# A SwiGLU feed-forward on one core: units in four parts, the down projection of one part traced beside the gate and up of the next, and 19 of 22 units by seven block products in four PSUM banks

## The chip, the cores and the metric

The kernel runs on one core of one Trainium2 chip. The time is device microseconds for one execution; the profiled execution is a further one, taken by the hardware profiler. Engines are named as in the profile: PE is TensorE (PEld its weight loads), DVE is VectorE, ACT is ScalarE, POOL is GpSimd, SP is SyncE, which here only issues DMA.

## The reference

Two layers of a decoder trunk over 512 tokens of width 1024, float32. Each layer is a mixer of 16 attention heads of three kinds, a SwiGLU feed-forward, and a gated embedding; a norm stands ahead of each and one at the end. The change is in the feed-forward:

```python
D_FF = 2816
...
    hn = rms_norm(h, norm_ffn[i])
    h = h + (jax.nn.silu(hn @ w_ffn_gate[i]) * (hn @ w_ffn_up[i])) @ w_ffn_down[i]
    gate = jax.nn.sigmoid(rms_norm(h, norm_ple[i]) @ w_ple_gate[i])
    h = h + (p[i] @ w_ple_proj[i]) * gate
```

## The kernel before

**Precision by splitting.** Every float32 operand is split in a high and a low part, and each product is three matmuls (high x high, high x low, low x high: `mm3`, lines 223 to 227). Weights arrive by DMA as float32 (`load_raw`, tile `wraw`, four buffers of 512 KB), ACT casts the high part (line 200, or 451), and DVE or GpSimd subtracts it for the low part (line 203, or 452). The result is a tile `whl`, of which there are five. In the feed-forward the general helper `halves` gives every second subtraction to GpSimd.

**Gate and up.** The 2816 hidden columns are taken in 11 pairs of 128 (`fp` 0 to 10), and a pair has two units, gate and up: 22 units a layer. Unit weights are the stationary operand, the normed activations (512 tokens) the moving one, so a unit gives two 128 x 512 results, transposed. A *plain* unit (tile `gu`) has 8 row blocks x 2 halves x 3 = 48 matmuls of 512 columns. Pair 0 is plain with 256 columns at a time, twice as many, since the second half of the tokens is normed later.

**Units by seven.** `seven` (lines 427 to 478, tile `st`) sees a unit as a 2 x 2 block product and makes it with seven block products instead of eight (Winograd's form). The sums of activations that it needs are built once a layer (`operand_sums`); the sums of weights are made for each unit by DVE (`combine`, line 437, in tile `T`). The products run in the order 1, 7, 5, 2, 6, 4, 3. Each is 4 x 3 = 12 matmuls of 256 columns, 84 in all. Four combinations, seven casts on ACT, three splits on GpSimd (products 1, 2, 3) and four on DVE, three copies of partial results on ACT and five additions on DVE (lines 466 to 477), which read PSUM, go with a unit. Results are tiles `gs`, two a unit, of the tag `p`, which has six buffers.

Pairs 1 to 10 take the plain way where `2 * fp + wi` divides by 3 (`wi` is 0 for gate, 1 for up), which are 7 of 20 units, and the other 13 go by seven. PSUM has eight banks in four tags: d two, s three, t two, o one. Gate units by seven take d, d, s, s and up units s, o, t, t.

**The product and the down projection.** For each pair gate is passed through Silu, DVE multiplies gate and up (line 1222), ACT casts (1223) and GpSimd subtracts (1224): the tile `hid`, which is split and ready to be the stationary operand of the down projection. This is done in two parts: pairs 0 to 5, then the down projection of their 12 row blocks; pairs 6 to 10, then that of their 10. A down projection has two halves of 512 columns (`project`), each with four accumulators, one for each 128 tokens, and each row block needs 4 x 3 = 12 matmuls of 512 columns. The first half uses banks d, d, s, s and the second s, t, t, o. DVE adds the accumulators into `h` (`add_h`, line 1109). Ahead of the last half `between` starts the embedding stage, whose input transposes, splits and loads are traced with a lead of 200 instructions.

**The order.** The program is traced in one order, and a planner then places each instruction on its engine by priority (the place in the trace, or ahead of it in a `prio` block) as tiles and inputs come free in its own reckoning. `weave` traces several generators in turn, by the share of each that is done; the mixer uses it. Engines run their own queues in order and wait for one another by semaphores, PE's included. SP issues the loads.

Of the kernel before, what the change touches and what calls it, by code (L numbers as in the profile page):

```python
# [10 lines left out]
F32 = mybir.dt.float32  # L11
# [8 lines left out]
P = 128  # L20
# [22 lines left out]
def hybrid_trunk_kernel(  # L43
# [28 lines left out]
    def bank(tag, shape=(P, 512), dt=F32, name=None):  # L72
        bufs = {"d": 2, "s": 3, "t": 2, "o": 1}[tag]
        return ps.tile(list(shape), dt, name=name or f"ps_{tag}", tag=tag, bufs=bufs)
# [44 lines left out]
    def run(*gens):  # L119
        for g in gens:  # L120
            for _ in g:
                pass
# [68 lines left out]

    turn, lo_turn = [0], [3]

    def load_raw(view, k, c):
        raw = wpool.tile([P, 1024], F32, name="wraw", tag="wraw", bufs=4)
        nc.sync.dma_start(raw[:, :k * c].rearrange("p (k c) -> p k c", k=k), view)
        return raw

# [8 lines left out]
        halves(raw, whl, lo, n)  # L207
        return whl

    def weights(w, kts, c0, c, per):  # L210


        step = min(1024 // c // per * per, len(kts))
        for i in range(0, len(kts), step):
            n = min(step, len(kts) - i)
            src = w[kts[i] * P:(kts[i] + n) * P, c0:c0 + c].rearrange("(k p) c -> p k c", p=P)
            raw = load_raw(src, n, c)
            for j in range(0, n, per):
                t = split(raw, j * c, per * c).rearrange("p t (k c) -> p t k c", c=c)
                for kk in range(per):  # L220
                    yield t[:, 0, kk], t[:, 1, kk]
# [4 lines left out]
        te.matmul(acc, lhsT=ll, rhs=rh, start=False, stop=stop, skip_group_check=True)  # L226
        return i

    def project(act, w, kts, c0, c, evac, tags="ddss", tail=2):

        pack = c <= 256
        if pack:
            b2 = [bank(t, (P, 2, 256), name=f"acc{j}") for j, t in enumerate(tags[:2])]
            accs = [b2[tt // 2][:, tt % 2, :c] for tt in range(NT)]
        else:
            accs = [bank(t, name=f"acc{tt}")[:, :c] for tt, t in enumerate(tags)]
        n = len(kts)
        first = None  # L240
        ws = []
        for i, wt in enumerate(weights(w, kts, c0, c, 2 if pack else 1)):
            k = kts[i]
            if i >= n - tail:
                ws.append((k, wt))
                continue
            for tt in range(NT):
                start = i == 0 and not (pack and tt % 2)
                if i == 0 and pack and tt % 2:
                    with tc.issue_after(first):  # L250
                        mm3(accs[tt], act(k, 0, tt), act(k, 1, tt), *wt, False, False)
                else:
                    m = mm3(accs[tt], act(k, 0, tt), act(k, 1, tt), *wt, start, False)
                    if i == 0:
                        first = m.ins
            yield 12 * c
        for tt in range(NT):
            for j, (k, wt) in enumerate(ws):
                start = n == tail and j == 0
                if start and pack and tt % 2:  # L260
                    with tc.issue_after(first):
                        mm3(accs[tt], act(k, 0, tt), act(k, 1, tt), *wt, False, j == tail - 1)
                else:
                    m = mm3(accs[tt], act(k, 0, tt), act(k, 1, tt), *wt, start, j == tail - 1)
                    if start:
                        first = m.ins

            for t in () if pack and tt % 2 == 0 else (tt - 1, tt) if pack else (tt,):
                with prio(OFE):
                    evac(t, accs[t])  # L270
            yield 3 * tail * c
# [152 lines left out]
            return xact(4 * kh + k, half)[:, t * 256:(t + 1) * 256]  # L424
        return left

    def seven(left, w, c0, tags, done):


        raw = [load_raw(w[kh * 512:(kh + 1) * 512, c0:c0 + 256].rearrange("(k p) c -> p k c", p=P), 4, 256)  # L430
               .rearrange("p (k c) -> p k c", k=4) for kh in range(2)]
        b11, b12, b21, b22 = (raw[i][:, :, j * P:(j + 1) * P] for i in range(2) for j in range(2))
        T, acc, part = {}, {}, {}

        def combine(n, a, b):
            T[n] = t = f(swtile("T")).rearrange("p (k c) -> p k c", k=4)
            ve.tensor_tensor(t, a, b, op=ALU.subtract)
            return t

        def right(n):  # L440
            if n in (1, 2, 3):
                return (b11, b21, b22)[n - 1]
            return combine(n, *{7: lambda: (b22, b12), 5: lambda: (b12, b11), 6: lambda: (b22, T[5]),
                                4: lambda: (b21, T[6])}[n]())

        out = [ptile(f"gs{j}") for j in range(2)]
        for n in (1, 7, 5, 2, 6, 4, 3):
            src = right(n)
            whl = wpool.tile([P, 2, 560], F32R, name="whl", tag="whl", bufs=5)[:, :, :512] \
                .rearrange("p t (k c) -> p t k c", k=4)  # L450
            se.activation(whl[:, 0], src, AF.Copy)  # L451
            (ge if n in (1, 2, 3) else ve).tensor_tensor(whl[:, 1], src, f(whl[:, 0]), op=ALU.subtract)  # L452

            a = {1: 0, 6: 0, 2: 1, 7: 2, 4: 2, 5: 3, 3: 3}[n]
            if a not in acc:
                acc[a] = bank(tags[a], name=f"st{a}")[:, :256]
            for k in range(4):
                mm3(acc[a], whl[:, 0, k], whl[:, 1, k], left(n, 0, k), left(n, 1, k),
                    k == 0 and n in (1, 2, 7, 5), k == 3 and n in (6, 2, 4, 3))
            with prio(OFE):  # L460
                if n in (1, 7):
                    part[n] = eftile("part")
                    se.activation(part[n], acc[a], AF.Copy)
                elif n == 5:
                    part[n] = eftile("part")
                    ve.tensor_tensor(part[n], part[7], acc[a], op=ALU.add)
                elif n == 2:
                    ve.tensor_tensor(out[0][:, :256], part[1], acc[a], op=ALU.add)
                elif n == 6:
                    ve.tensor_tensor(out[1][:, 256:], part[5], acc[a], op=ALU.add)  # L470
                    part[n] = eftile("part")
                    se.activation(part[n], acc[a], AF.Copy)
                elif n == 4:
                    ve.tensor_tensor(out[0][:, 256:], part[6], acc[a], op=ALU.add)
                    done(0, out[0])
                else:
                    ve.tensor_tensor(out[1][:, :256], part[6], acc[a], op=ALU.add)
                    done(1, out[1])

    allk = list(range(KD))  # L480

# [722 lines left out]
    def feed_forward(i, add_h, between):  # L1204
# [7 lines left out]
        def units(fp):  # L1212
# [21 lines left out]

            for wi, w in enumerate((w_ffn_gate[i], w_ffn_up[i])):

                if fp and (2 * fp + wi) % 3:
                    seven(left[0], w, fp * 256, ("ddss", "sott")[wi], (gate_done, up_done)[wi])
                    continue
                accs = [bank(t, name=f"gu{wi}{j}") for j, t in enumerate(("dd", "ss" if fp == 0 else "to")[wi])]  # L1240
                ws = enumerate(weights(w, allk, fp * 256, 256, 2))
                first = []
                if fp == 0:

                    ws = list(ws)
                    part(w, accs, ws, slice(0, 256))
                    with tc.issue_after(first[1]):
                        part(w, accs, ws, slice(256, 512))
                else:
                    part(w, accs, ws, slice(0, 512))  # L1250
                for j in range(2):
                    if wi:
                        up_done(j, accs[j])
                    else:
                        gate[j] = sg = etile("sg")
                        se.activation(sg, accs[j], AF.Silu)
                if fp == 0 and wi == 0:
                    left.append(operand_sums(xact))


        parts = range(0, 6), range(6, NF // 2)
        for fps in parts:
            for fp in fps:
                units(fp)
            end = fps is parts[-1]
            kts = list(range(2 * fps[0], 2 * fps[-1] + 2))
            for c, tags in ((0, "ddss"), (512, "stto")):
                if end:
                    if c:
                        between()  # L1270
                    else:
                        load_gain(norm_ple[i])
                run(project(hact, w_ffn_down[i], kts, c, 512, add_h(c, end), tags=tags,
                            tail=4 if end and c else 2))


    def layer_embedding(i):
# [164 lines left out]
```

## Time and profile before

| | |
|---|---|
| Median of 3 runs | 1540.3 us (1536.8 to 1544.35) |
| Profiled execution, its own time | 1536.46 us |
| Its span, first to last instruction | 1534.5 us |
| Mean granted TensorE clock | 0.997 |
| Instructions | 25780, of them 9562 matmuls |
| DMA | 134.74 MB, mean 88 GB/s |

The page gives an engine's busy time as a share of the span. Matmuls are pipelined, so that a busy PE says that matmuls are under way, not that they could not be closer together; the spacing of their starts says that. The timeline gives starts and durations in us from the start of the span.

### The profile page before, as it was taken

The numbers are of one execution on the slowest core, as the hardware profiler recorded it, in microseconds if no ns is written. First come the engines' busy times: TensorE is split into PE (matmuls) and PEld (weight loads), VectorE is DVE, ScalarE is ACT, GpSimd is POOL, SyncE is SP. The second block draws the span as 40 slices with busy tenths as digits, with TensorE's granted clock in tenths as the row PEclk, the third lists the DMA queues.
The fourth block names the chain that finished last, engine by engine and source line by source line (L and its number), as shares of the span: only waits on it lengthen the run. The fifth ranks groups of instructions, "written<-read, shape, count | busy, mean of one in ns | idle before, by whom it ended". The sixth has DMA issues, their size and how long they took to land.

```text
span 1534.5 us, 25780 instructions
## 1 busy us (share of the span) xinstructions
PE 1482.6 (97%) x9562; PEld 1305.5 (85%) x9562; DVE 988.7 (64%) x1910; ACT 813.3 (53%) x1743; POOL 649.1 (42%) x675
## 2 busy tenths in 40 slices
PE   6999999998999999999999999999899999999998
PEld 6898887878999899988988888778699988998888
DVE  7577868769775267624376878786787733674253
ACT  5477678555454244533365767776455532454243
POOL 3413455454545244432224235555444532455223
PEclk9999999999999999999999999999999999999999
DMA  5521321131433324331225131112122332324321
GB/s 181 134 63 43 84 69 35 49 97 42 124 97 111 96 79 123 118 127 64 83 70 145 52 83 50 54 37 83 56 89 91 106 109 89 111 90 144 110 70 56
DMA packets 114461, 134.74 MB, mean 88 GB/s; under 512 B 6864, under 2 KB 91936, under 8 KB 114336
## 3 DMA queue, kind: packets, MB, share of 16 engines
q1 hardware_dynamic: 114336, 133.10, 28.6%
q8 instruction: 76, 1.25, 0.3%
q14 instruction: 49, 0.40, 0.1%
HBM read 122.59 MB, written 2.10 MB: 81 GB/s over the span
## 4 chain that ended last, share of the span: by engine, by line
PE 81%; DVE 8%; ACT 4%; POOL 3%; issue 2%; DMA 1%; SPq 0%; POOLq 0%; ACTq 0%; DVEq 0%
PE acc L224 6%; PE acc L225 6%; PE acc L226 6%; PE st L225 6%; PE st L226 6%; PE st L224 6%; PE gu L225 4%; PE gu L226 4%; PE gu L224 4%; PE pTp L892 2%; PE sc L871 2%; PE no L1088 2%; PE accr L224 2%; PE accr L225 2%; PE ge L224 2%; PE accr L226 2%
## 5 line engine op out<-in xcount | busy, mean ns | idle before, releaser
L203 POOL TENSOR_TENSOR whl<-wraw,whl 128x512 fp32r<-128x512 f32 (+2 forms) x196 | 267.0, 1367 | 439.1 <-ACT whl L200 412.1
L200 ACT ACTIVATE whl<-wraw 128x512 fp32r<-128x512 f32 (+2 forms) x312 | 195.3, 631 | 249.9 <-PE acc L226 135.0
L203 DVE TENSOR_TENSOR whl<-wraw,whl 128x512 fp32r<-128x512 f32 x116 | 104.8, 904 | 167.2 <-ACT whl L200 166.8
L452 POOL TENSOR_TENSOR whl<-wraw,whl 128x512 fp32r<-128x512 f32 x78 | 115.8, 1491 | 144.4 <-ACT whl L451 144.3
L224 PE MATMUL acc<-whl,hid 128*128 128x512 f32 x352 | 139.1, 395 | 0.0
L225 PE MATMUL acc<-whl,hid 128*128 128x512 f32 x352 | 139.0, 395 | 0.0
L226 PE MATMUL acc<-whl,hid 128*128 128x512 f32 x352 | 138.8, 394 | 0.0
L225 PE MATMUL gu<-xT,whl 128*128 128x512 f32 (+1 forms) x352 | 125.0, 355 | 0.0
L226 PE MATMUL gu<-xT,whl 128*128 128x512 f32 (+1 forms) x352 | 124.8, 355 | 0.0
L224 PE MATMUL gu<-xT,whl 128*128 128x512 f32 (+1 forms) x352 | 124.6, 356 | 0.0
L452 DVE TENSOR_TENSOR whl<-T,whl 128x512 fp32r<-128x512 f32 x104 | 100.3, 971 | 30.1 <-ACT whl L451 29.8
L225 PE MATMUL st<-X,whl 128*128 128x256 f32 x416 | 116.9, 281 | 0.0
L224 PE MATMUL st<-X,whl 128*128 128x256 f32 x416 | 116.6, 280 | 0.0
L226 PE MATMUL st<-X,whl 128*128 128x256 f32 x416 | 116.6, 280 | 0.0
L884 POOL TENSOR_SCALAR p<-p,rc,gt 128x128 f32<-128x128 f32 (+3 forms) x128 | 79.3, 629 | 72.7 <-DVE rc L882 28.8
L879 ACT ACTIVATE p<-sc,mx 128x128 f32<-128x128 f32 (+3 forms) x160 | 83.4, 532 | 10.2 <-DVE mx L876 7.6
L897 ACT ACTIVATE pT<-pTp 128x512 fp32r<-128x512 f32 (+2 forms) x120 | 61.8, 526 | 49.8 <-PE pTp L892 48.5
L451 ACT ACTIVATE whl<-T 128x512 fp32r<-128x512 f32 x104 | 64.3, 625 | 44.7 <-PE gu L226 24.1
L225 PE MATMUL st<-xT,whl 128*128 128x256 f32 x312 | 87.6, 281 | 0.0
L226 PE MATMUL st<-xT,whl 128*128 128x256 f32 x312 | 87.5, 280 | 0.0
L224 PE MATMUL st<-xT,whl 128*128 128x256 f32 x312 | 87.5, 280 | 0.0
L898 DVE TENSOR_TENSOR pT<-pTp,pT 128x512 fp32r<-128x512 f32 (+2 forms) x120 | 70.6, 596 | 24.9 <-ACT pT L897 23.9
(337 smaller groups left out, 4630.9 us busy)
## 6 DMA issues: line engine op xcount, KB each, us to landing
wraw<-in_w_ffn_gate_dram SPq DMA_DIRECT2D x44, 512.0 KB, 3.5
wraw<-in_w_ffn_up_dram SPq DMA_DIRECT2D x44, 512.0 KB, 4.1
wraw<-in_w_ffn_down_dram SPq DMA_DIRECT2D x44, 512.0 KB, 3.7
wraw<-in_w_in_dram SPq DMA_DIRECT2D x36, 512.0 KB, 3.7
wraw<-in_w_out_dram SPq DMA_DIRECT2D x16, 512.0 KB, 3.7
wraw<-in_w_ple_gate_dram SPq DMA_DIRECT2D x16, 512.0 KB, 3.4
sw<-nq SPq DMA_DIRECT2D x32, 128.0 KB, 2.4
wraw<-in_w_in_dram SPq DMA_DIRECT2D x8, 280.0 KB, 2.9
```

Of the source, the lines that this page charges most:

```text
L200: se.activation(whl[:, 0], raw[:, lo:lo + n], AF.Copy)
L203: eng.tensor_tensor(whl[:, 1], raw[:, lo:lo + n], f(whl[:, 0]), op=ALU.subtract)
L224: i = te.matmul(acc, lhsT=lh, rhs=rh, start=start, stop=False, skip_group_check=True)
L225: te.matmul(acc, lhsT=lh, rhs=rl, start=False, stop=False, skip_group_check=True)
L226: te.matmul(acc, lhsT=ll, rhs=rh, start=False, stop=stop, skip_group_check=True)
L451: se.activation(whl[:, 0], src, AF.Copy)
L452: (ge if n in (1, 2, 3) else ve).tensor_tensor(whl[:, 1], src, f(whl[:, 0]), op=ALU.subtract)
L871: te.matmul(s[:, c:c + w], lhsT=lhsT, rhs=rhs, start=(j == 0), stop=False, skip_group_check=True)
L879: se.activation(e[:, u * n:(u + 1) * n], s[:, u * n:(u + 1) * n], AF.Exp, bias=mx[:, u:u + 1], accum_out=sm[:, u:u + 1])
L884: ge.tensor_scalar(e[:, u * n:(u + 1) * n], e[:, u * n:(u + 1) * n], rc[:, u:u + 1], gates[u] if gates else 1.0, op0=ALU.mult, op1=ALU.mult)
L897: se.activation(hi, src, AF.Copy)
L898: ve.tensor_tensor(lo, src, f(hi), op=ALU.subtract)
```

## The change

The feed-forward is cut in four parts, pairs 0 to 2, 3 to 5, 6 to 8 and 9 to 10, instead of two. The first part's units are traced alone. The units of each further part are woven with the down projection of the part ahead of it, a product of a unit and a row block of the down projection at a time, by share. The last part's down projection stands alone at the end. For the weave `seven` and `units` become generators, and `down` is a generator with the old body.

All units by seven use banks s, s, s, o. The down projection uses d, d, t, t in both halves, and plain units use d, d and t, t. Of pairs 1 to 10 only the up unit of pair 1 stays plain, so that 19 of 22 units go by seven.

The down weights are loaded one row block at a time (256 KB, tile `wrow`) into the six buffers of the tag `p`, which the results of `seven` use as well, instead of two at a time (512 KB) into `wraw`.

```diff
-    def load_raw(view, k, c):
-        raw = wpool.tile([P, 1024], F32, name="wraw", tag="wraw", bufs=4)
+    def load_raw(view, k, c, one=False):
+        raw = ptile("wrow") if one else wpool.tile([P, 1024], F32, name="wraw", tag="wraw", bufs=4)
...
-    def weights(w, kts, c0, c, per):
+    def weights(w, kts, c0, c, per, one=False):
-        step = min(1024 // c // per * per, len(kts))
+        step = 1 if one else min(1024 // c // per * per, len(kts))
...
-            raw = load_raw(src, n, c)
+            raw = load_raw(src, n, c, one)
...
-    def project(act, w, kts, c0, c, evac, tags="ddss", tail=2):
+    def project(act, w, kts, c0, c, evac, tags="ddss", tail=2, one=False):
...
-    def seven(left, w, c0, tags, done):
+    def seven(left, w, c0, done):
...
-                acc[a] = bank(tags[a], name=f"st{a}")[:, :256]
+                acc[a] = bank("ssso"[a], name=f"st{a}")[:, :256]
...
                     ve.tensor_tensor(out[1][:, :256], part[6], acc[a], op=ALU.add)
                     done(1, out[1])
+            yield 12 * 256
...
-                if fp and (2 * fp + wi) % 3:
-                    seven(left[0], w, fp * 256, ("ddss", "sott")[wi], (gate_done, up_done)[wi])
+                if fp and (fp, wi) != (1, 1):
+                    yield from seven(left[0], w, fp * 256, (gate_done, up_done)[wi])
                     continue
-                accs = [bank(t, name=f"gu{wi}{j}") for j, t in enumerate(("dd", "ss" if fp == 0 else "to")[wi])]
+                accs = [bank(t, name=f"gu{wi}{j}") for j, t in enumerate(("dd", "tt")[wi])]
...
-        parts = range(0, 6), range(6, NF // 2)
-        for fps in parts:
-            for fp in fps:
-                units(fp)
-            end = fps is parts[-1]
+                yield 48 * 512
+
+        def down(fps, end=False):
             kts = list(range(2 * fps[0], 2 * fps[-1] + 2))
-            for c, tags in ((0, "ddss"), (512, "stto")):
+            for c in (0, 512):
                 if end:
                     if c:
                         between()
                     else:
                         load_gain(norm_ple[i])
-                run(project(hact, w_ffn_down[i], kts, c, 512, add_h(c, end), tags=tags,
-                            tail=4 if end and c else 2))
+                yield from project(hact, w_ffn_down[i], kts, c, 512, add_h(c, end), tags="ddtt",
+                                   tail=4 if end and c else 2, one=True)
+
+        parts = range(0, 3), range(3, 6), range(6, 9), range(9, NF // 2)
+        for n, fps in enumerate(parts):
+            streams = [(chain(*[units(fp) for fp in fps]), len(fps) * 42 * 1024)]
+            if n:
+                streams.append((down(parts[n - 1]), len(parts[n - 1]) * 24 * 1024))
+            weave(*streams)
+        run(down(parts[-1], True))
```

## Rows read from the trace of the kernel before

**Rows 1.** The page: engines over the whole span; below, the last chain by engine.

```profile
PE 1482.6 (97%) x9562; PEld 1305.5 (85%) x9562; DVE 988.7 (64%) x1910; ACT 813.3 (53%) x1743; POOL 649.1 (42%) x675
...
PE 81%; DVE 8%; ACT 4%; POOL 3%; issue 2%; DMA 1%; SPq 0%; POOLq 0%; ACTq 0%; DVEq 0%
```

**Rows 2.** Windows, first layer's feed-forward: length; PE, PEld, DVE, ACT, POOL busy; clock; DMA.

```profile
345.36:376.53 31.17, 26.33 (x209) 25.80 (x208) 29.37 (x27) 15.25 (x26) 13.04 (x12) 0.95 0.16 51
376.53:479.05 102.52, 102.52 (x734) 96.36 (x733) 77.52 (x104) 54.08 (x102) 54.52 (x38) 1.00 0.33 100
479.05:545.64 66.59, 66.59 (x290) 54.18 (x289) 19.56 (x26) 16.18 (x26) 19.41 (x14) 1.00 0.32 101
545.64:649.58 103.94, 103.94 (x700) 95.68 (x698) 68.70 (x92) 50.82 (x95) 50.90 (x35) 1.00 0.35 107
649.58:708.58 59.00, 58.06 (x259) 46.40 (x258) 18.59 (x30) 22.36 (x45) 20.61 (x23) 1.00 0.32 109
```

**Rows 3.** Timeline of PE: the first matmul of four blocks that follow one another.

```profile
376.53 0.28 PE L224 MATMUL st<-xT,whl 128*128 128x256 f32 x1
...
386.43 0.39 PE L224 MATMUL gu<-xT,whl 128*128 128x512 f32 x1
...
397.50 0.28 PE L224 MATMUL st<-xT,whl 128*128 128x256 f32 x1
...
417.28 0.39 PE L224 MATMUL gu<-xT,whl 128*128 128x512 f32 x1
```

**Rows 4.** Groups by line, whole span: busy us, mean ns, then idle before and releasers.

```profile
L452 POOL TENSOR_TENSOR whl<-wraw,whl 128x512 fp32r<-128x512 f32 x78 | 115.8, 1491 | 144.4 <-ACT whl L451 144.3
...
L452 DVE TENSOR_TENSOR whl<-T,whl 128x512 fp32r<-128x512 f32 x104 | 100.3, 971 | 30.1 <-ACT whl L451 29.8
...
L203 POOL TENSOR_TENSOR whl<-wraw,whl 128x512 fp32r<-128x512 f32 (+2 forms) x196 | 267.0, 1367 | 439.1 <-ACT whl L200 412.1 <-DVE dup L500 10.2 <-PE cmp L607 6.4
...
L203 DVE TENSOR_TENSOR whl<-wraw,whl 128x512 fp32r<-128x512 f32 x116 | 104.8, 904 | 167.2 <-ACT whl L200 166.8
...
L437 DVE TENSOR_TENSOR T<-wraw,T 128x512 f32<-128x512 f32 x52 | 53.8, 1034 | 1.2
...
L437 DVE TENSOR_TENSOR T<-wraw 128x512 f32<-128x512 f32 x52 | 45.5, 877 | 26.7 <-DMA wraw<-in_w_ffn_gate_dram 17.0 <-DMA wraw<-in_w_ffn_up_dram 8.9
...
L1224 POOL TENSOR_TENSOR hid<-gs,hid 128x512 fp32r<-128x512 f32 x28 | 40.4, 1460 | 29.6 <-ACT hid L1223 29.6
...
L1109 DVE TENSOR_TENSOR h<-h,acc 128x512 f32<-128x512 f32 x32 | 21.9, 686 | 14.8 <-PE acc L226 14.8
...
L1223 ACT ACTIVATE hid<-gs 128x512 fp32r<-128x512 f32 x28 | 16.9, 624 | 23.3 <-DVE gs L1222 23.3
...
L1222 DVE TENSOR_TENSOR gs<-gs,gs 128x512 f32<-128x512 f32 x12 | 13.4, 1114 | 0.1
...
L474 DVE TENSOR_TENSOR gs<-part,st 128x256 f32<-128x256 f32 x26 | 10.8, 414 | 1.3
```

**Rows 5.** The splits of units by seven (line 452): ns min/median/max, first and last start.

```profile
L452 DVE TENSOR_TENSOR whl<-T,whl x104: 677/693/1797, 375.5 to 1389.2; 128x512 fp32r<-128x512 f32 x104
...
L452 POOL TENSOR_TENSOR whl<-wraw,whl x78: 1291/1322/1766, 369.4 to 1390.4; 128x512 fp32r<-128x512 f32 x78
```

**Rows 6.** The page's DMA issues: count, KB each, median us from issue to landing.

```profile
wraw<-in_w_ffn_down_dram SPq DMA_DIRECT2D x44, 512.0 KB, 3.7
...
wraw<-in_w_in_dram SPq DMA_DIRECT2D x8, 280.0 KB, 2.9
```

**Rows 7.** Timeline at the first layer's feed-forward end: a transpose on PE, additions and split on DVE.

```profile
702.26 0.44 PE L382 MATMUL xnT<-ident,xn 128*128 128x128 f32 x2 [0.40 <-DVE h L1109]
...
705.28 0.68 DVE L1109 TENSOR_TENSOR h<-h,acc 128x512 f32<-128x512 f32 x1
...
710.24 0.67 DVE L1109 TENSOR_TENSOR h<-h,acc 128x512 f32<-128x512 f32 x1
...
717.16 0.69 DVE L390 TENSOR_TENSOR xT<-xnT,xT 128x512 fp32r<-128x512 f32 x1
```

More of the change, by code (lines that the diff above doesn't have):

```diff
@@ L241, in project @@
         ws = []
-        for i, wt in enumerate(weights(w, kts, c0, c, 2 if pack else 1)):
+        for i, wt in enumerate(weights(w, kts, c0, c, 2 if pack else 1, one)):
             k = kts[i]
```

## Prediction

> **What bounds the kernel now.** I read the page's engine shares first. TensorE is busy for 97% of the span, VectorE for 64%, and the chain that ended last runs over TensorE for 81% [rows 1]. The 97% says only that matmuls overlap one another; whether TensorE ever waits is read from where the matmuls start. So I cut one layer's feed-forward into stretches at the first matmul of each block [rows 2]: 345.36 is the first gate matmul of unit pair 0, 376.53 the first seven-product matmul, 479.05 the first down projection, 545.64 pair 6, 649.58 the second down projection. From 376.53 to 649.58 TensorE has no hole and the granted clock is 1.00. Only the opening stretch (4.8 us idle, waiting for the norm) and the last (0.9 us) have any, and the change works at neither hole. The second layer repeats the pattern.
>
> Then the price of a unit [rows 3]. A unit by seven products starts at 376.53 and the next block at 386.43: 9.90 us for 84 matmuls of 256 columns. A plain unit runs from 386.43 to 397.50: 11.07 us for 48 of 512 columns. Two units by seven in a row take 19.78 us, 9.89 each. Now rebuild the stretches: the first has seven units by seven and three plain, 7 x 9.89 + 3 x 11.07 = 102.4 us against 102.52; the other has six and four, 103.6 against 103.94. Nothing but matmul starts is left in them. So feed-forward time here is a sum of matmul pitches, and only fewer or shorter matmuls can shorten it.
>
> **The change, part by part.** *Six units per layer go from plain to seven products* (13 of 22 becomes 19 of 22). Each saves 11.07 - 9.89 = 1.18 us of TensorE; twelve of them save 14.1 us. That is the ceiling: no other matmul disappears, and the down projection keeps its 576 per layer at 66.59 / 288 = 0.231 us.
>
> The Trainium skill has a figure that speaks against this ("TensorE: Matmul & The Clock Gate", Back-to-back issue gap): a sustained stream is said to cost about 131 ns per matmul at 512 columns and 81 ns at 128, so that narrow matmuls are dear. By it even 81 ns would make a unit by seven 84 x 0.081 = 6.8 us against 48 x 0.131 = 6.3 us, and the change would lose. The trace disagrees: 0.231 and 0.118 us.
>
> The break-even is a 256-column pitch of 48/84 = 0.57 of the 512-column one, and rows 3 give 0.51 (9.90/84 against 11.07/48). I give a loss by pitch no chance worth counting.
>
> *What VectorE must do for it.* This is the real question, because a unit by seven costs VectorE [rows 4] four combinations (two at 0.877, two at 1.034), four splits at 0.971 and five evictions at 0.414 us: 9.78 us beside 9.89 us of TensorE. Alone, with the gate-up product on top, units by seven are bound by VectorE. Before, every third unit was plain and gave VectorE time to catch up. Now the down projection is to do that. Per layer, pairs 3 to 10 (16 units) run beside the down projection of pairs 0 to 8: TensorE 16 x 9.89 + 9 x 11.10 = 258.1 us. VectorE: 16 x 9.78 = 156.5; 16 products of gate and up at 1.114 = 17.8; 36 splits of down weights, every other one on VectorE, 18 x 0.904 = 16.3; 24 additions into h at 0.686 = 16.5. Sum 207.1 us, 80%. In the stretch from 376.53 it is 77.52 / 102.52 = 76% [rows 2], and nothing waits. GpSimd: 48 x 1.491 + 18 x 1.367 + 16 x 1.460 = 119.5 us, 46%, against 54.52 / 102.52 = 53%. ScalarE stays near half. So on the averages the cover is as good as before, and I cost it at nothing. If the cover goes, for instance in pair 2 where two units by seven stand alone, VectorE needs 19.6 + 2.2 us against 19.8; but pairs 0 to 2 are the same work in the same order as now, and there 397.50 to 417.28 ran without a wait.
>
> The additions into h double, from 16 to 32 a layer; they are in the sum above.
>
> *Four banks instead of eight.* Each unit by seven now takes the same s, s, s, o, so an accumulator must be evicted before the next unit opens it. The tightest is the o bank: product 3, the last of a unit, closes it, and the next unit opens it with its product 5, two products (2.8 us) later. The eviction takes 0.414 us plus what runs ahead on VectorE. Below: one operation of 0.69 us, 1.1 us in all, no wait. Above: two at the slowest split, 1.80 us [rows 5], 4.0 us, so 1.2 us for each of 38 units, 46 us. In the woven stretch a down step of 12 matmuls (2.77 us) falls between every three or four products and widens the slack. The median split is 0.693 us [rows 5], so I take nothing and keep the upper end for a rival.
>
> *Down on the banks d, d, t, t in both halves.* Before, the two halves had different banks. Now the second half's tile 3 opens 9 matmuls (2.1 us) after the first half's tile 3 ended; the addition into h takes 0.69 us plus at most one slow operation of 1.80 us, 2.5 us. So 0 to 0.4 us at each of 14 seams, 0 to 5.6 us; other streams' matmuls stand ready, so I take 0.
>
> *The t banks at the layer's end.* The next norm's transposes need t. Now the first of them goes into the middle of the down projection, at 702.26, between the matmuls of tiles 1 and 2 [rows 7]. With tiles 2 and 3 themselves in t, it can't go before tile 2 is added, which now ends at 705.96: 3.7 us later at worst. At best nothing, because what ends the phase is tile 3 (added at 710.24, its last operand written at 717.85 [rows 7]), and without transposes in between tile 3 ends earlier. Between 0 and 3.7 us a layer I take 1.5, nearer the end that the last operand supports: 3 us in all. The preparation of the embedding inputs is traced in the same place with the same lead; its ScalarE and VectorE work lies in the last stretch, where they are busy 22.36 and 18.59 of 59.00 us [rows 2], and that stretch now has 22 us of down projection left instead of 55. I count it inside the same 3.7 us.
>
> *Loads.* 44 down loads of 512 KB become 88 of 256 KB on the same queue, into the six p tiles that they share with the results of the units by seven (up to four live). A load lands in at most 2.9 us (the 280 KB row, [rows 6]), the cast and split take 0.63 (as the 0.624 of the hidden cast, rows 4) + 1.367: 4.9 us a slot, and one is wanted every 258.1 / 36 = 7.2 us. One slot would do; nothing.
>
> *Last down part.* It has four steps of rows instead of ten. Its rows 20 and 21 need the last hidden pair: eviction 0.414 + product 1.114 + cast 0.624 + GpSimd 1.460 = 3.6 us [rows 4], under 24 matmuls of rows 18 and 19 (5.5 us). Nothing.
>
> **Sum.** The profiled execution took 1536.5 us (span 1534.5). 1536.5 - 14.1 + 3.0 = 1525.4. The median of the three runs is 1540.3, 3.8 above it, so the forecast for the median is 1529 us, 0.7% faster. A difference under 0.5% (7.7 us) is about what a measurement of this kernel can't tell from no change.
>
> **The rivals.** *A, the forecast*: matmul pitches are saved and little is given back: -14.1 plus 0 to 8 us, or 2 us less if tile 3's chain gains: 1524 to 1534 (both bounds of the seams and the t banks together, 5.6 + 7.4 = 13 us, would be 1539, inside the range below). Chance 0.65. For it: the holes are absent now and VectorE's share hardly rises.
>
> *B, the four banks*: TensorE waits at the opening of a unit for an eviction queued behind one slow VectorE operation. At 0.3 us for each of 38 units it gives back 11.4 us: 1540.3 - 14.1 + 11.4 = 1538. At 0.37 us the gain is gone. For it: the banks halve, and an operation ahead can take 1.80 us. Against: the slack of 2.8 us. Chance 0.22, all within 0.5%.
>
> *C, VectorE becomes the bound, and the kernel slower.* Of its 207.1 us, 162 operations with both operands in SBUF (128 in units by seven, 16 products, 18 splits) take 157.3 us, 0.97 us on average; alone they take 0.69 and beside GpSimd up to 1.80 [rows 5]. TensorE's 258.1 us is reached when the average is (258.1 - 49.8) / 162 = 1.29, the gain is eaten at 1.33, and at 1.40 the layer loses 18.5 us: 1540.3 - 14.1 + 37 = 1563. For it: combinations and splits of all units now lean on VectorE. Against: GpSimd's share falls from 53% to 46%. Chance 0.08.
>
> The Trainium skill says why these stretch ("SBUF — State Buffer", Who interferes with whom): a VectorE instruction with two SBUF inputs and a GpSimd one that reads SBUF exclude each other for the whole instruction. The spread in rows 5 agrees. Taken as one resource by that rule, the stretch from 376.53 has 68 x 0.69 + 37 x 1.29 = 94.6 of 102.5 us and the woven one 162 x 0.69 + 82 x 1.29 = 217.6 of 258.1: the rule speaks against C.
>
> *D, the weave doesn't happen*: the instruction order is settled by a planner, and if it runs the down steps ahead as their inputs allow, the units by seven stand alone at the end. Then VectorE sets them: 16 x 9.78 + 17.8 = 174.3 against 158.2 us, 16 us a layer; 1540.3 - 14.1 + 32 = 1558. Against: in rows 3 the units run in the order in which they are traced. Chance 0.05.
>
> **How the numbers follow.** The time is A's, 1529. The range takes A and B and leaves out C and D (0.13): 1523 to 1541. Faster by over 0.5% means under 1532.6; A gives 0.62 of its 0.65 there, its upper end and B give 0.25 within 0.5%, C and D 0.13 slower.
>
> **What would show it.** Right: 38 x 84 = 3192 matmuls of units by seven where there were 2184, at 0.118 us pitch, no TensorE hole in the woven stretch, VectorE near 80% there, its splits near 0.97 us, and about 7 us less per layer from the first gate matmul to the embedding's first one. Wrong: holes before product 1, 7 or 5 of a unit released by an eviction (B); splits above 1.3 us and TensorE waiting for them (C); long runs of one stream alone (D); a later last operand of the norm (my 3 us).

## The result, and the profile after

The changed kernel takes 1583.3 us (median of four runs, 1578.9 to 1587.1) against 1540.5 us for the kernel before beside it: 1.0278 times as long, 95% interval 1.0260 to 1.0295. The forecast was 1529 us in a range of 1523 to 1541. The profiled execution took 1586.0 us, with a span of 1584.2 us.

The page of the kernel after, with its engines over the span, the last chain by engine, three groups of TensorE and the row of the new load:

```profile
PE 1490.8 (94%) x9994; PEld 1324.2 (84%) x9994; DVE 1091.2 (69%) x2074; ACT 835.3 (53%) x1815; POOL 680.7 (43%) x687
...
PE 60%; DVE 9%; DMA 9%; POOL 8%; ACT 7%; issue 5%; SPq 1%; POOLq 0%; ACTq 0%; DVEq 0%
...
L224 PE MATMUL st<-X,whl 128*128 128x256 f32 x608 | 170.9, 281 | 1.3 <-DVE gs L477 1.3
...
L224 PE MATMUL acc<-whl,hid 128*128 128x512 f32 x352 | 128.8, 407 | 26.9 <-ACT whl L200 26.7
L225 PE MATMUL acc<-whl,hid 128*128 128x512 f32 x352 | 142.3, 404 | 10.2 <-POOL whl L203 8.0
...
wrow<-in_w_ffn_down_dram SPq DMA_DIRECT2D x88, 256.0 KB, 4.6
```

TensorE's share went from 97% to 94%, and the chain that ended last has 9% of DMA in it where it had 1% [rows 1]. The second and third groups are the new fact: down matmuls (`acc`) waited 26.9 + 10.2 us for their weights, 26.7 of it for ScalarE's cast (L200). The first group answers to rival B: over the whole kernel the units by seven waited 1.3 us for an eviction (DVE L477).

One layer's feed-forward of the kernel after in stretches, as in [rows 2]: pair 0 from 346.19, units by seven alone (and the one plain unit) from 378.39, the weave from 425.34, the last down part from 705.67 to 742.14, the first matmul of the embedding's gate that reads the new norm. Columns are length; busy time of PE, PEld, DVE, ACT, POOL; granted clock; DMA share and GB/s.

```profile
346.19:378.39 32.20, 27.35 (x209) 26.84 (x208) 29.81 (x28) 15.39 (x26) 13.35 (x12) 0.89 0.19 58
378.39:425.34 46.95, 42.58 (x314) 40.11 (x312) 31.49 (x46) 21.38 (x42) 22.93 (x16) 1.00 0.35 107
425.34:705.67 280.33, 264.97 (x1765) 239.93 (x1765) 188.70 (x260) 117.19 (x227) 120.19 (x80) 0.99 0.29 93
705.67:742.14 36.47, 32.61 (x174) 26.21 (x173) 24.84 (x38) 20.00 (x42) 18.79 (x21) 1.00 0.40 130
```

The sum is 396.0 us; the kernel before needs 372.2 us between the same two matmuls (345.36 to 717.57). In the weave TensorE stands idle for 280.33 - 264.97 = 15.4 us, in the stretch ahead of it 4.4 us.

What the first hole looks like, on four queues of the kernel after. SP's load queue:

```profile
417.15 0.37 SPq L196 DMA_DIRECT2D wraw<-in_w_ffn_up_dram  x1
418.43 0.74 SPq L196 DMA_DIRECT2D wraw<-in_w_ffn_gate_dram  x1
419.22 1.34 SPq L196 DMA_DIRECT2D wrow<-in_w_ffn_down_dram  x2
```

VectorE, an addition that gives a result `gs` of pair 2's last unit its first value:

```profile
417.52 0.42 DVE L470 TENSOR_TENSOR gs<-part,st 128x256 f32<-128x256 f32 x1 [0.90 <-PE st L226]
```

ScalarE (in brackets: idle time ahead, and what ended it):

```profile
420.19 0.63 ACT L1224 ACTIVATE hid<-gs 128x512 fp32r<-128x512 f32 x1 [1.76 <-DVE gs L1223]
424.66 0.63 ACT L200 ACTIVATE whl<-wrow 128x512 fp32r<-128x512 f32 x1 [3.84 <-DMA wrow<-in_w_ffn_down_dram]
```

TensorE:

```profile
421.45 0.28 PE L226 MATMUL st<-xT,whl 128*128 128x256 f32 x1
425.34 0.80 PE L224 MATMUL acc<-whl,hid 128*128 128x512 f32 x1 [3.62 <-ACT whl L200]
```

Read from the end: the first down matmul starts at 425.34, where the last matmul before it, which ends the first product of pair 3's gate unit, started at 421.45; and it waited for the cast. The cast started at 424.66 after 3.84 us of waiting for a load `wrow`. That load had been issued at 419.22, right behind a load of unit weights at 418.43, and not before pair 2's last result was first written, at 417.52. `wrow` and `gs` are tiles of one tag, p, with six buffers, of which results hold up to four at a time; the load took none of them until the results traced ahead of it had theirs. (Pair 3's first two results are declared ahead of it too, but first written later, and it did not wait for those: the place that counts seems to be that of a tile's first write.) On SP's queue it stands behind unit loads that wait for their own buffers: the one at 417.15 is the second of a pair whose first went out at 407.30. So what is late is the load's place in the order.

### The profile page after: what moved, and what is told of

Its sections match the earlier page's. It is cut to its first block, busy times and chain, and to the rows that moved or that the text cites. A ratio compares the mean times of both kernels' runs of the same rounds, so it can differ in the third digit from the quotient of the medians.

```text
span 1584.2 us, 26933 instructions
## 1 busy us (share of the span) xinstructions
PE 1490.8 (94%) x9994; PEld 1324.2 (84%) x9994; DVE 1091.2 (69%) x2074; ACT 835.3 (53%) x1815; POOL 680.7 (43%) x687
## 3 DMA queue, kind: packets, MB, share of 16 engines
q8 instruction: 79, 1.29, 0.3%
## 4 chain that ended last, share of the span: by engine, by line
PE 60%; DVE 9%; DMA 9%; POOL 8%; ACT 7%; issue 5%; SPq 1%; POOLq 0%; ACTq 0%; DVEq 0%
DMA wrow<-in_w_ffn_down_dram 8%; PE st L224 4%; PE st L225 4%; PE st L226 4%; PE acc L225 4%; PE acc L226 4%; PE acc L224 4%; POOL whl L203 3%; POOL whl L452 2%; PE pTp L893 2%; PE sc L872 2%; PE no L1089 2%; PE accr L224 2%; PE ge L224 2%; PE accr L225 2%
## 5 line engine op out<-in xcount | busy, mean ns | idle before, releaser
L203 POOL TENSOR_TENSOR whl<-wraw,whl 128x512 fp32r<-128x512 f32 (+2 forms) x128 | 176.3, 1386 | 272.4 <-ACT whl L200 247.1
L452 DVE TENSOR_TENSOR whl<-T,whl 128x512 fp32r<-128x512 f32 x152 | 163.8, 1093 | 33.8 <-ACT whl L451 32.9
L224 PE MATMUL st<-X,whl 128*128 128x256 f32 x608 | 170.9, 281 | 1.3 <-DVE gs L477 1.3
L225 PE MATMUL st<-X,whl 128*128 128x256 f32 x608 | 170.7, 281 | 0.0
L226 PE MATMUL st<-X,whl 128*128 128x256 f32 x608 | 170.5, 281 | 0.0
L224 PE MATMUL acc<-whl,hid 128*128 128x512 f32 x352 | 128.8, 407 | 26.9 <-ACT whl L200 26.7
L225 PE MATMUL acc<-whl,hid 128*128 128x512 f32 x352 | 142.3, 404 | 10.2 <-POOL whl L203 8.0
L200 ACT ACTIVATE whl<-wraw 128x512 fp32r<-128x512 f32 (+2 forms) x176 | 109.6, 630 | 56.7 <-PE accT L226 18.9
L225 PE MATMUL st<-xT,whl 128*128 128x256 f32 x456 | 128.1, 281 | 0.0
L224 PE MATMUL st<-xT,whl 128*128 128x256 f32 x456 | 128.0, 281 | 0.0
L226 PE MATMUL st<-xT,whl 128*128 128x256 f32 x456 | 127.8, 280 | 0.0
L224 PEld LDWEIGHTS st<-X,whl 128*128 128x128 f32 x608 | 114.3, 188 | 5.1 <-DVE gs L477 1.7
L225 PEld LDWEIGHTS st<-X,whl 128*128 128x128 f32 x608 | 114.4, 188 | 3.5
L226 PEld LDWEIGHTS st<-X,whl 128*128 128x128 f32 x608 | 114.8, 189 | 0.0
L451 ACT ACTIVATE whl<-T 128x512 fp32r<-128x512 f32 x152 | 90.7, 623 | 33.2 <-PE st L226 20.0
L203 POOL TENSOR_TENSOR whl<-wrow,whl 128x512 fp32r<-128x512 f32 x44 | 63.1, 1433 | 97.8 <-ACT whl L200 97.8
L224 PEld LDWEIGHTS acc<-whl,hid 128*128 128x128 f32 x352 | 63.9, 190 | 42.9 <-ACT whl L200 33.1
L451 ACT ACTIVATE whl<-wraw 128x512 fp32r<-128x512 f32 x114 | 70.7, 625 | 54.8 <-PE st L226 34.7
L1225 POOL TENSOR_TENSOR hid<-gs,hid 128x512 fp32r<-128x512 f32 x40 | 61.9, 1549 | 75.4 <-ACT hid L1224 75.1
```

The source lines that it names most:

```text
L200: se.activation(whl[:, 0], raw[:, lo:lo + n], AF.Copy)
L203: eng.tensor_tensor(whl[:, 1], raw[:, lo:lo + n], f(whl[:, 0]), op=ALU.subtract)
L224: i = te.matmul(acc, lhsT=lh, rhs=rh, start=start, stop=False, skip_group_check=True)
L225: te.matmul(acc, lhsT=lh, rhs=rl, start=False, stop=False, skip_group_check=True)
L1225: ge.tensor_tensor(hid[:, 1, j, :], sg, f(hid[:, 0, j, :]), op=ALU.subtract)
```

## The experiments

The theory: the down loads come late because they take their buffers behind the results of the units by seven, in the tag p. Within it four causes can be told apart: the order in which one tag's buffers are handed out; too few buffers; a load that the planner places too late; and loads of 256 KB instead of 512. The rival theory: units by seven with so few plain ones among them are themselves too much for VectorE or for the load buffers, and the weave makes it no better. All ratios are to the kernel before, run beside it (medians 1539.7 to 1541.0 us), with 95% intervals.

**e1: the down loads in the tag e.**

```diff
-        raw = ptile("wrow") if one else wpool.tile([P, 1024], F32, name="wraw", tag="wraw", bufs=4)
+        raw = etile("wrow") if one else wpool.tile([P, 1024], F32, name="wraw", tag="wraw", bufs=4)
```

> The down weights get four buffers of their own (the tag e, nearly idle in the feed-forward) instead of the six p buffers that they share with the results of the units by seven; nothing else changes. Late loads (theory 1): in the changed kernel some 29 of the 31 us of TensorE holes per layer stand before a down matmul, ScalarE waits 25 us per layer for a down weight to land, and the loads go out in pairs right after a unit's weights. With own buffers four loads are under way ahead, so most holes close: 1583 - 2 x 20 to 29, that is 1525 to 1543 us. VectorE bound (theory 2): units by seven leave VectorE and ScalarE too little room and the down weights' cast and split come late whenever their data land: 1570 to 1583 us.

1537.5 us, 0.9976 [0.9963, 0.9989]. One word takes 46 us off. The first down load now goes out at 371.59:

```profile
371.59 0.97 SPq L196 DMA_DIRECT2D wrow<-in_w_ffn_down_dram  x2
```

The loss is in the shared tag. (The 29 us of holes a layer in the expectation are too many: the page of the kernel after has 26.9 + 10.2 us ahead of down matmuls for both layers together.)

**e5: the down loads in pairs of row blocks, in the tag `wraw`.** Everything else of the change stays.

```diff
-                                   tail=4 if end and c else 2, one=True)
+                                   tail=4 if end and c else 2)
```

> The woven kernel with the down weights loaded as before the change, two row blocks of 512 KB at a time into the four buffers that gate and up use too. Theory 1 in the form that the p buffers alone make the loads late: one load stands a whole unit ahead again, 1530 to 1550 us. Theory 1 in the form that the in-order load queue does it (a load that waits for a buffer holds back all behind it): gate and up now lose buffers to down as well, 1560 to 1600 us. Theory 2: no change, 1575 to 1590 us.

1526.9 us, 0.9914 [0.9885, 0.9942], the fastest.

**e3: four parts, but each down projection after its own units, nothing woven.** The down loads stay in p.

```diff
-            if n:
-                streams.append((down(parts[n - 1]), len(parts[n - 1]) * 24 * 1024))
-            weave(*streams)
+            run(*[g for g, _ in streams[:1]])
+            if n < len(parts) - 1:
+                run(down(parts[n]))
```

> Four parts, four banks, 19 of 22 units by seven, but each part's down projection after its units instead of beside the next part's. Theory 1 (late down loads are the whole loss): the units then pay at most VectorE's excess; if VectorE keeps up, 1540 - 14 + 0 to 6 us, 1526 to 1532. Theory 2 (VectorE is the bound where units by seven stand in a row): per pair 2 x 9.78 + 2.23 = 21.8 us of VectorE against 19.8 us of TensorE, nine pairs a layer, +18 - 7 = +11 us a layer, about 1562 us; four banks on top would make it more.

1599.8 us, 1.0386 [1.0345, 1.0428]. The feed-forwards take 401.3 and 403.9 us, against 396.0 and 392.5 in the kernel after. So it is not the weave that loses: without it the kernel is slower still. Both numbers of the expectation are missed, and so they are in e4, the next run: neither counts the turn of the buffers for unit weights, which e11 finds in e4.

**e4: the kernel before, only with the 19 units by seven** (two parts, old banks, old loads).

```diff
-                if fp and (2 * fp + wi) % 3:
+                if fp and (fp, wi) != (1, 1):
```

> The kernel before with one line changed: 19 instead of 13 of 22 units by seven, with the old two parts, old banks (d, d, s, s and s, o, t, t) and old loads. If VectorE keeps up in long rows of units by seven, the full saving: 1540 - 14 = 1526 us. If VectorE is the bound there: 9 pairs a layer at 21.8 instead of 19.8 us, 1562 us. Against the run without the weave it shows what the four banks cost.

1589.1 us, 1.0317 [1.0287, 1.0347]. Its stretch of eight units by seven in a row, and what VectorE's combinations waited for in it (us in total, times, longest):

```profile
401.90:493.76 91.86, 84.00 (x673) 80.55 (x672) 69.96 (x106) 47.16 (x96) 48.39 (x32) 1.00 0.31 88
```

```profile
DVE T L437 <- DMA wraw<-in_w_ffn_up_dram: 9.5, 3, 3.4
DVE T L437 <- DMA wraw<-in_w_ffn_gate_dram: 7.8, 3, 3.5
```

A unit takes 91.86 / 8 = 11.48 us, longer than the 11.07 us of a plain one [rows 3], so more units by seven alone only lose. VectorE is 76% busy, hence not the bound; it waits 17.3 us for loads. What holds these is tried in e11.

Here both theories seemed to hold something, and the next four kernels take the shared tag apart.

**e12: the results moved out instead of the loads**, so that the down loads have p's six buffers for themselves.

```diff
-        out = [ptile(f"gs{j}") for j in range(2)]
+        out = [etile(f"gs{j}") for j in range(2)]
```

> The mirror of the run with own buffers: the down weights stay alone in the six p buffers, and the results of the units by seven move to the four e buffers. Theory 1a (the buffers of one tag are handed out in traced order, so a load that shares the tag can't be issued until the results traced ahead of it have got theirs, which is when VectorE first writes them): the loads now run six ahead and the holes before down matmuls close, 1525 to 1540 us, with something lost if four buffers are tight for results of which up to four live. Theory 1b (there are too few buffers for loads and results together): the same for the loads, but the results are now short, 1540 to 1560 us.

1529.8 us, 0.9923 [0.9893, 0.9953]. The load queue of this kernel, and the page's row for the load:

```profile
347.28 15.73 SPq L196 DMA_DIRECT2D wrow<-in_w_ffn_down_dram  x6
```

```profile
wrow<-in_w_ffn_down_dram SPq DMA_DIRECT2D x88, 256.0 KB, 2.9
```

Six down loads go out between 347.28 and 363.01, sixty us and more before the first down matmul, and over the whole kernel a load lands in a median of 2.9 us. The load and its tag are those of the kernel after. What ended the idle time of ScalarE ahead of the line of the casts (L200) from 425 to 705 us, in the kernel after (total us, times):

```profile
  DMA wrow<-in_w_ffn_down_dram: 19.8, 12
  PE acc L226: 3.3, 1
```

and in this kernel:

```profile
  PE acc L226: 20.0, 12
  issue: 5.0, 5
```

The wait of 19.8 us for the load is gone; what ScalarE waits for now is a matmul, that is a free weight tile.

**e8: eight buffers in p** (and two in e, for the room).

```diff
-        return upool.tile([P, 512], F32, name=name, tag="e", bufs=4)
+        return upool.tile([P, 512], F32, name=name, tag="e", bufs=2)
...
-        return upool.tile([P, 512], F32, name=name, tag="p", bufs=6)
+        return upool.tile([P, 512], F32, name=name, tag="p", bufs=8)
```

> The changed kernel with eight instead of six p buffers (two of the e buffers are given up for the memory; the feed-forward hardly uses them, the mixer may lose a little). Theory 1b (too few p buffers): two more loads can be under way, holes before down matmuls fall by half or more, 1535 to 1565 us. Theory 1a (order within the tag): more buffers don't help, since the next load stands behind a result that is not made yet; 1578 to 1590 us.

1596.3 us, 1.0355 [1.0283, 1.0427], above both ranges of the expectation. Instructions that touch `wrow` in this kernel (ns min/median/max, first and last start), and the total and count of the waits for its load:

```profile
L196 SPq DMA_DIRECT2D wrow<-in_w_ffn_down_dram x88: 327/424/1179, 423.3 to 1498.1; - x88
...
  DMA wrow<-in_w_ffn_down_dram: 58.0, 34
```

More buffers do not bring the load forward: the first is issued at 423.3 us, 72.4 us after the first gate matmul, against 73.0 in the kernel after. Its feed-forwards take 394.1 and 394.9 us, as there (396.0 and 392.5); of the 5.8 us by which its profiled span is longer, all but 0.6 lie outside them.

That buffers are not short can be read in the kernel after itself. At the start of the feed-forward p still holds the normed rows (`xn`); their readers on TensorE, and the first writes of the results of units by seven:

```profile
L382 PE MATMUL xnT<-ident,xn x32: 270/273/446, 339.8 to 359.3; 128*128 128x128 f32 x32
...
L468 DVE TENSOR_TENSOR gs<-part,st x38: 405/420/424, 384.7 to 1480.2; 128x256 f32<-128x256 f32 x38
```

From 359.6 to 384.7 all six buffers are empty, and no down load takes one; in e12 six loads have them by 363. In the same time loads for the embedding stage go out, which have another tag (e) and are traced, with a lead of 200 instructions, behind all down loads but those of the last half:

```profile
370.07 0.97 SPq L1289 DMA_DIRECT2D ple<-in_p_dram  x2
```

**e2: the load with a lead of 300 instructions in the planner's order.**

```diff
-        nc.sync.dma_start(raw[:, :k * c].rearrange("p (k c) -> p k c", k=k), view)
+        with prio(300 if one else 0): nc.sync.dma_start(raw[:, :k * c].rearrange("p (k c) -> p k c", k=k), view)
```

> The changed kernel with each down load traced with a lead of 300 instructions. If the loads are late because they stand late in the order of priorities, the lead brings them out ahead of the units' loads: 1530 to 1560 us. Theory 1a: the lead changes the priority, not the order within the tag: 1578 to 1588 us, with down weights landing as late as before.

1588.4 us, 1.0304 [1.0257, 1.0350]. The same view of this kernel:

```profile
L196 SPq DMA_DIRECT2D wrow<-in_w_ffn_down_dram x88: 327/406/1041, 421.2 to 1496.4; - x88
...
  DMA wrow<-in_w_ffn_down_dram: 50.4, 30
```

Asking for the load earlier does nothing either; it starts at 421.2 us, 73.3 us after the first gate matmul. Neither number nor priority decides, then. That one tag's buffers are handed out in the order of the trace is what agrees with e2 and e8, where the load stands behind the results and does not move, with e12 and e1, where it stands behind none that are made late and goes, and with the empty buffers.

**e6: one row block at a time, as in the change, but in the tag `wraw`.**

```diff
-        raw = ptile("wrow") if one else wpool.tile([P, 1024], F32, name="wraw", tag="wraw", bufs=4)
+        raw = wpool.tile([P, 1024], F32, name="wrow" if one else "wraw", tag="wraw", bufs=4)
```

> Down weights one row block at a time (256 KB) as in the change, but in the four buffers of gate and up, in whose tag all that is traced ahead is a load as well. Size of the load as the cause: it stays slow, above 1560 us. Theory 1a: the loads go out a unit ahead, most holes close; a row block takes a whole buffer, so it may trail the run with pairs (1527 us): 1527 to 1545 us.

1531.4 us, 0.9942 [0.9917, 0.9968]. Loads of 256 KB are not the cause.

**e5 again, with more runs**, as the version that beats both kernels.

> The woven kernel with down weights loaded in pairs into the four buffers of gate and up, once more with more rounds: 1527 us, 0.86% faster than the kernel before, the saving of twelve units less nothing. It stands beside the next run for a difference of a few us.

1528.2 us against 1539.9, 0.9914 [0.9893, 0.9935]. The same stretches as above, in this kernel, the first issue of a down load, and two VectorE groups in the weave:

```profile
348.44:380.96 32.52, 27.67 (x210) 27.15 (x209) 29.78 (x28) 15.39 (x26) 13.29 (x12) 0.90 0.19 57
380.96:424.12 43.16, 42.41 (x314) 40.15 (x313) 32.91 (x47) 22.97 (x44) 21.99 (x16) 1.00 0.34 96
424.12:680.50 256.38, 256.38 (x1765) 238.24 (x1764) 184.31 (x259) 121.28 (x228) 117.38 (x83) 1.00 0.34 103
680.50:714.20 33.70, 31.86 (x175) 26.36 (x174) 22.85 (x37) 18.33 (x39) 17.42 (x20) 1.00 0.48 156
```

```profile
L196 SPq DMA_DIRECT2D wraw<-in_w_ffn_down_dram x44: 367/368/368, 409.9 to 1436.5; - x44
```

```profile
L452 DVE TENSOR_TENSOR whl<-T,whl 128x512 fp32r<-128x512 f32 x62 | 61.9, 1002 | 25.3 <-ACT whl L451 24.9
...
L203 DVE TENSOR_TENSOR whl<-wraw,whl 128x512 fp32r<-128x512 f32 x19 | 16.0, 842 | 12.6 <-ACT whl L200 12.1
```

In the weave TensorE's busy time is the length of the stretch, 256.38 us. The first down load goes out at 409.9 us, 14 us ahead of the first down matmul. The feed-forward takes 365.8 us, and 365.4 in the second layer, against 372.2 and 372.4 before.

**e10: e5, with the last down part on the banks of before.**

```diff
-                yield from project(hact, w_ffn_down[i], kts, c, 512, add_h(c, end), tags="ddtt",
+                yield from project(hact, w_ffn_down[i], kts, c, 512, add_h(c, end), tags=("stto" if c else "ddss") if end else "ddtt",
```

> The same, with the last down projection of a layer, which stands alone, on the old banks (d, d, s, s, then s, t, t, o), so that the t banks come free earlier for the next norm's transposes. If the prediction's 1.5 us a layer for the t banks was right: 3 us less, about 1524 us. If tile 3's chain sets the end anyway: no difference, 1527 us.

1531.9 us, 0.9943 [0.9924, 0.9962]. The first transpose of the norm does come earlier, at 700.91 us instead of 703.65 in e5, and nothing is gained: the feed-forwards take 368.6 and 367.7 us.

**e11: e4 with five buffers for unit weights** (and two in e, for the room).

```diff
-        raw = wpool.tile([P, 1024], F32, name="wraw", tag="wraw", bufs=4)
+        raw = wpool.tile([P, 1024], F32, name="wraw", tag="wraw", bufs=5)
```

> The run with 19 units by seven in the old order, with a fifth weight buffer (two e buffers given up for it). There eight units by seven in a row took 11.5 us each instead of 9.9, while VectorE was busy for only 76% and waited 47 us a layer for gate and up weights to land. If the turn of the four weight buffers is what stretches rows of units by seven (a buffer is free only after a unit's last split, and the next load takes 4 us from there): the fifth takes 10 to 25 us off each layer, 1540 to 1570 us. If VectorE's own work or order is: 1580 to 1592 us.

1554.6 us, 1.0088 [1.0054, 1.0122]. The stretch that answers to that of e4:

```profile
403.49:486.85 83.36, 81.34 (x674) 79.79 (x672) 78.65 (x106) 47.88 (x96) 49.43 (x32) 1.00 0.33 98
```

83.36 / 8 = 10.42 us a unit, and VectorE is busy for 94% and no longer waits for a load. So in e4 the turn of the four load buffers cost about a microsecond a unit. By its share VectorE is the next bound behind it; that was not tried.

## Why the prediction was wrong

**The step that failed is *Loads*:** "One slot would do; nothing." It counted slots and the time for which each is held, as if any free buffer of p could be taken, and put at nothing what cost 57 us. None of the signs of being wrong that it listed names a down load. It listed the results of the units by seven as sharers of the six tiles and did not ask in which order sharers get theirs. The load is traced behind the results of the units woven with it, and e12, e2 and e8 show the rest: with the results out of the tag the loss is gone; with the results in it neither a lead nor more buffers help, and six empty buffers are not used. Then three queues pass the lateness on. SP issues the load right behind a load of unit weights; ScalarE, in order, stands at the cast until the load lands, with casts for the units queued behind it (L451 at 425.20 follows directly); TensorE stands at the down matmul. I had priced the landing at no more than 2.9 us, which is a median in [rows 6]; its median here is 4.6 us.

**What it costs.** A layer's weave in the kernel after is 280.33 - 256.38 = 24.0 us longer than in e5: 15.4 us of TensorE idle and 8.6 us more busy time, part of which is a lower clock behind holes (last section). The stretches ahead of and behind the weave add 3.8 and 2.8 us, the opening takes 0.3 less, and over the layer it is 396.0 - 365.8 = 30.2 us, in the second layer 392.47 - 365.43 = 27.0. Sum 57.2 us, beside 55.1 us between the medians.

**The saving was right.** With the load out of the way (e5) a layer's feed-forward is 6.4 and 7.0 us shorter, 13.4 us in all, against 14.1 predicted (5.8 and 6.5 us in e12, which keeps the change's loads of 256 KB). The prediction's 576 down matmuls a layer are 528 (22 row blocks of 24); nothing in its sum hangs on that. The median shows 11.75 us of it. Between the two profiled executions it is only 6.6 us of span, since outside the feed-forward e5 is 6.8 us longer there, 3.1 us of them already ahead of the first gate matmul. What causes that stays open; the kernel before alone spreads over 7.5 us. The figure of the Trainium skill that spoke against units by seven ("TensorE: Matmul & The Clock Gate", Back-to-back issue gap: in a sustained stream about 131 ns a matmul at 512 columns and 81 ns at 128) is not borne out: e5 has the 19 units by seven, and its feed-forward is shorter.

**VectorE's cover: right; priced too high as a sum.** Predicted for the weave were 207.1 us of VectorE in 258.1 us (80%) and 119.5 us of GpSimd. In e5 they are 184.31 in 256.38 us (72%) and 117.38. Added row by row, as the prediction added them, VectorE's operations there come to 196.7 us: neighbours overlap by some hundredths of a microsecond in the record, which the busy time counts once. The rest of the difference is mostly in the combinations, 52.9 us for the 60 in the stretch where 61.2 were priced for 64. The splits of units by seven average 1.002 us there, and 0.971 was priced [rows 4]. In the kernel after they are at 1.167:

```profile
L452 DVE TENSOR_TENSOR whl<-T,whl 128x512 fp32r<-128x512 f32 x64 | 73.6, 1167 | 15.2 <-ACT whl L451 14.8
```

but VectorE is busy for 188.70 of 280.33 us (67%), and all its operations with two inputs in SBUF average 0.95 us (149.7 us for 158 in the weave), so rival C (from 1.29 over all of them) is not what happened. The rule of the Trainium skill by which I had spoken against C ("SBUF — State Buffer", Who interferes with whom: a VectorE instruction with two SBUF inputs and a GpSimd one that reads SBUF exclude each other) agrees with that: TensorE had no hole in e5's weave. How much the cover matters e4 shows: without it a unit takes 11.48 us, more than D's 10.9 us for VectorE alone, because the loads take their turn as well; with a fifth buffer (e11) it is 10.42.

**The four banks: right at nothing.** 1.3 us over the kernel; rival B fell. The d, d, t, t seams: no hole in e5's weave, so nothing.

**The t banks at the layer's end: not confirmed.** I took 3 us; with the old banks at the end (e10) the time is 3.7 us longer, if anything. The mechanism is seen (the first transpose waits for tile 2's addition), but it does not set the end.

**Rival D did not happen.** The weave runs as traced, twelve down matmuls after every three or four products of a unit. Its other half, units by seven alone, is e4's case, and it does lose there.

What stays open: why e1 is 9 to 11 us slower than e5; 8.0 us of it lie in the feed-forwards (369.65 and 369.59 us). Its tag e also serves the embedding stage's inputs, traced behind most of the down loads, which would hold these as p held the loads; that was not tried by itself. Nor was the order in which buffers are handed out seen directly; it is inferred from which edits move the load.

## What to carry to other kernels

In this kernel a prefetch was only as early as its buffer: give it a tag in which nothing that is made late stands ahead of it in the trace, and when a load moves to another tag, ask what is traced there before it, not how many buffers there are. When a transfer is late although its pool has room, compare its issue time with the writes of its neighbours in the pool before touching priorities or buffer counts. And a cheaper product that leans on another engine has to be priced with its cover taken away as well (e4): here the matmuls saved 1.18 us a unit and the neighbour engines' turn could cost 1.6.

## What the runs showed of the hardware

In the kernel after TensorE paid twice for the hole ahead of the first down matmul. Around it, from 421.45, the granted clock of four stretches (the number behind the engines):

```profile
417.50:421.45 3.95, 3.95 (x36) 3.95 (x35) 2.60 (x5) 1.01 (x2) 1.46 (x2) 1.00 0.68 192
421.45:425.34 3.89, 0.27 (x3) 0.07 (x1) 0.06 (x2) 0.68 (x2) 1.17 (x1) 0.99 0.61 214
425.34:428.50 3.16, 3.16 (x8) 2.48 (x9) 3.12 (x4) 2.30 (x5) 2.09 (x2) 0.50 0.00 0
428.50:432.00 3.50, 3.50 (x25) 3.28 (x24) 2.21 (x2) 0.63 (x2) 0.97 (x1) 0.98 0.00 0
```

After 3.9 us in which TensorE did next to nothing the granted clock is 0.50, its lower level of 1.2 GHz, over the next 3.2 us, and then 0.98. The matmuls of the same kernel show it in their starts:

```profile
427.22 0.63 PE L226 MATMUL acc<-whl,hid 128*128 128x512 f32 x1
427.64 0.63 PE L225 MATMUL acc<-whl,hid 128*128 128x512 f32 x1
...
429.03 0.40 PE L224 MATMUL acc<-whl,hid 128*128 128x512 f32 x1
429.27 0.39 PE L225 MATMUL acc<-whl,hid 128*128 128x512 f32 x1
```

Down matmuls start 0.42 us apart at the lower clock and 0.23 to 0.24 us apart at the upper one. Seven starts at the longer pitch are some 1.4 us beside the hole's 3.9.

A down load of 256 KB lands in a median of 2.9 us in e12 (3.3 us for those from 425 to 700 us), where most go out more than a microsecond behind the start of the load before them, and in 4.6 us in the kernel after (4.5 in the same time), where most go out within about a microsecond of the start of a load of 512 KB; around the first of these the DMA engines are 0.68 and 0.61 busy. That the two loads share the engines is the likely reason; it was not tried by itself.
